# The residual's gate: products on ACT, POOL and DVE, summed over partitions by PE

## The chip, the cores and the metric

The kernel runs on one core of a Trainium2 chip. The metric is the device time of one execution in microseconds. Before the change the median of three runs is 2271.47 us (2270.25 to 2272.49).

The engines of a core are named as in the profile: PE multiplies matrices (PEld is its load of the stationary operand), DVE and ACT and POOL work element by element, and SP issues most of the DMAs. A tile has 128 partitions; a matmul sums over the partitions of its two operands, the other engines work along the free dimension of each partition.

## The reference

One layer of a diffusion backbone on 128 context tokens and 256 latent tokens, with 2048 channels in fp32. What matters here is the adaptive modulation: two conditioning vectors (`c_ctx` for the context tokens, `c` for the latent ones) go through SiLU and one matrix of 2048 x 6144, which gives a shift, a scale and a gate for each stream.

```python
mod_ctx = (jax.nn.silu(c_ctx) @ ada_w[l] + ada_b[l])[None, None, :]
mod_lat = (jax.nn.silu(c) @ ada_w[l] + ada_b[l])[:, None, :]
...
shift, scale, gate = jnp.split(mod, 3, axis=-1)
h = _rmsnorm(x, norm_g) * (1.0 + scale) + shift
out, S_fin = _mixer(h, S0, rows, *mixer_w)
return x + gate * out, S_fin
```

`_mixer` ends with `merged = sigmoid(m_a) * y_a + sigmoid(m_b) * y_b` and `merged @ w_o`, where `y_a` and `y_b` are projections of the two branches by `w_out_a` and `w_out_b`. The gate is the last third of the 6144 columns: two vectors of 2048, each a product of a vector of 2048 with a matrix of 2048 x 2048. It is needed only where the output of `w_o` is multiplied by it and added to the residual.

## The kernel before, in words

All 384 tokens are handled together, with channels on the partitions and tokens in the free dimension. Every fp32 matrix product of the mixer is made of three matmuls of rounded parts (`mm3`): a weight tile and a data tile are each split into a rounded high part (`split`: a cast on ACT, tile `whi`) and the rest (a subtraction on DVE, tile `wlo`), and high x high, high x low and low x high are summed in PSUM.

The weight stream `ds_` (class `Stream`) walks over pairs of 128 output columns. For each pair, SP loads two halves of 1 MB (tile `raw`, two buffers), each half is split in two parts (three buffers of `whi` and of `wlo`), and each part feeds 24 matmuls. A count, `cnt`, is one `mm3` of the stream, three matmuls. The stream can carry a side generator, `side`, which is advanced once every so many counts; whatever it gives to PE stands at that place in PE's order. The order on PE is the order in which the program is written. The instructions of the other engines, and the DMAs, are ordered by a planner, in the main by the order of the program, but an instruction may come earlier on its engine when its inputs and its buffer are there. Once planned, each engine goes through its instructions in order.

The end of the kernel goes like this. The projection of branch B (`d_ob`, eight pairs) runs under the last scans. `load_ya` reads branch A's 16 tiles back from DRAM and splits them (`yah`, `yal`). Then comes the projection of branch A (`add_oa`, tile `d_oa`): eight pairs of 32 counts, 256 counts or 768 matmuls. After each column group of 128, `consume` multiplies the result by `sma`, adds `omb`, and splits the sum into `m_hi` and `m_lo`. Last come the products with `w_o` in column groups of 512, 512, 512, 256 and 256 (`acc`, `accl`), and `res_cols`, which multiplies by the gate, adds the residual and takes the final norm.

The gate is computed as side work of the projection of branch A, by `gate_rows` (line 994), in four quarters of 512 columns. For a quarter, `ada_rows` (line 277) reads four pieces of 1 MB of the matrix (tile `raw_adag`, three buffers) and makes four fp32 matmuls with each, in which the stationary operand `condw_gate` holds the two conditioning vectors in two of 32 columns. The four matmuls of a piece go to four groups of 32 rows of one PSUM tile (`pg`). ACT copies them to `m5g`, whose last row holds the bias, which a DMA from POOL's queue has brought (line 284). `m5g` is split (`m5h`, `m5l`), and for each stream two matmuls with a 0/1 selector (`sel_r`, lines 1008 and 1009) sum the rows and spread the sum over the 128 partitions (`pgb`); ACT copies that into `gate`. A quarter is eight steps of the generator, and one step is taken every five counts, so the gate lies in the first 160 of the 256 counts.

```python
if self.side is not None and self.cnt % 5 == 0:
    if next(self.side, 0) == 0:
        self.side = None
```

Of the kernel before, what the change touches and what calls it, by code (L numbers as in the profile page):

```python
# [9 lines left out]
F32 = mybir.dt.float32  # L10
F32R = mybir.dt.float32r
AF = mybir.ActivationFunctionType
ALU = mybir.AluOpType
AX = mybir.AxisListType

P = 128
D = 2048
# [18 lines left out]
NSEL = 99  # L36
# [20 lines left out]
def hybrid_step(ctx, tc, cst, x_prompt, x_sample, state_f, state_b, c, c_ctx, ada_w, ada_b, norm_g,  # L57
                w_in, mu_prev, mu_next, w0, w2, a0, a2, k_k, k_a, r_k, lnx_g, lnx_b, conv_w,
                w_out_a, w_out_b, w_o, final_g, y_prompt, y_sample, ns_f, ns_b):
    nc = tc.nc  # L60
    V, S, G, TE = nc.vector, nc.scalar, nc.gpsimd, nc.tensor

    win = w_in[0].rearrange("(k p) n -> p k n", p=P)
    adaw = ada_w[0].rearrange("(k p) n -> p k n", p=P)
# [15 lines left out]
    def mm3(out, wh, wl, xh, xl, start, stop):  # L80
        TE.matmul(out, wh, xh, start=start, stop=False)  # L81
        TE.matmul(out, wh, xl, start=False, stop=False)  # L82
        TE.matmul(out, wl, xh, start=False, stop=stop)  # L83

    def split(src, shape, th, tl, pool, nm, rows=P):
        hi = pool.tile(shape, F32R, tag=th, name=f"{th}_{nm}")
        lo = pool.tile(shape, F32R, tag=tl, name=f"{tl}_{nm}")
        S.copy(hi[0:rows], src)  # L88
        V.tensor_tensor(lo[0:rows], src, hi[0:rows].bitcast(F32), ALU.subtract)  # L89
        return hi, lo  # L90
# [20 lines left out]
    class Stream:  # L111
# [21 lines left out]
        def run(self):  # L133
            p = 0
            while True:
                self.extend(p)
                if p == len(self.pairs):
                    yield 0
                    continue
                tag, view, cols, xs, consume, before = self.pairs[p]  # L140
                if before is not None:
                    before()
                xh, xl = xs()
                ps = []
                nt = len(cols)
                for i in range(nt):
                    pst = pd.tile([P, 512], F32, tag="d", name=f"d_{tag}_{i}")
                    ps.append(pst[:, 0:T])
                for half in range(2):
                    self.load(2 * p + half)  # L150
                    self.load(2 * p + half + 1)
                    wt = self.ready.pop(2 * p + half)
                    self.ready[2 * p + half] = None
                    for q in range(2):
                        hi, lo = wt[q]
                        for i in range(nt):
                            sl = slice(i * P, (i + 1) * P)
                            for kk in range(4):
                                k = 8 * half + 4 * q + kk
                                mm3(ps[i], hi[:, kk, sl], lo[:, kk, sl], xh[k], xl[k],  # L160
                                    k == 0, k == KC - 1)
                                if half == 1 and q == 1 and kk == 3:
                                    consume(i, ps[i])
                                    if i == nt - 1:
                                        self.done.add(tag)
                                self.cnt += 1
                                if self.side is not None and self.cnt % 5 == 0:
                                    if next(self.side, 0) == 0:
                                        self.side = None
                                yield 1  # L170
                p += 1
# [27 lines left out]
    cT = cp.tile([P, 32], F32, tag="cT", name="cT")  # L199
# [27 lines left out]
    for i in range(3):  # L227
        pr = pp.tile([P, P], F32, tag=f"prow{i}", name=f"prow{i}")
# [35 lines left out]
    def cond_weights(pool, nm):  # L264
        cw = pool.tile([P, KC, 32], F32, tag="condw", name=f"condw_{nm}")
        V.memset(cw[:], 0.0)
        for s in range(2):
            V.tensor_copy(cw[:, :, s], cT[:, 16 * s:16 * s + 16])
        return cw

    def ada_load(rp, nm, cols, i, rbufs):
        raw = rp.tile([P, 4, 512], F32, tag="araw", name=f"raw_ada{nm}_{i}", bufs=rbufs)
        o = 0
        for c0, w in cols:
            nc.sync.dma_start(raw[:, :, o:o + w], adaw[:, 4 * i:4 * i + 4, c0:c0 + w])
            o += w
        return raw

    def ada_rows(cw, m5, cols, ps, get):


        o = 0
        for c0, w in cols:
            nc.gpsimd.dma_start(m5[NSEL - 1:NSEL, o:o + w], ada_b[0:1, c0:c0 + w])
            o += w
        for j in range(4):
            raw = get(j)
            for kk in range(4):
                TE.matmul(ps[32 * kk:32 * kk + 32, 0:512], cw[:, 4 * j + kk, :], raw[:, kk, :], start=j == 0, stop=j == 3)
            if j == 3:  # L290
                S.copy(m5[0:NSEL - 1, :], ps[0:NSEL - 1, 0:512])
            yield 1

    condw = cond_weights(pp, "pro")
    sel = cs[0:NSEL, C_SEL:C_SEL + 2]
# [74 lines left out]
    for g in range(8):  # L370
        m5 = pp.tile([NSEL, 512], F32, tag="m5", name=f"m5_{g}", bufs=2)
        pa = pps.tile([P, 512], F32, tag="ada", name=f"pada_{g}")
# [592 lines left out]
    og = ctx.enter_context(tc.tile_pool(name="og", bufs=1))  # L965
    po_ = ctx.enter_context(tc.tile_pool(name="po_", bufs=2, space=bass.MemoryType.PSUM))
    gate = og.tile([P, 2, D], F32, tag="gate", name="gate")
    ctx_oa = ExitStack()
    oa = ctx_oa.enter_context(tc.tile_pool(name="oa", bufs=1))

    def load_ya():
        box["yah"] = Rows(oa, "yh", "yah")
        box["yal"] = Rows(oa, "yl", "yal")
        yload(ya_d, box["yah"], box["yal"], "a", lambda nm: oa.tile([P, T], F32, tag="yst", name=nm, bufs=3))

    load_ya()
    cw2 = cond_weights(oa, "gate")
    sel_r = oa.tile([NSEL, 2], F32R, tag="sel_r", name="sel_r")
    S.copy(sel_r[:], sel)
    gcols = [[(2 * D + 512 * q, 512)] for q in range(4)]  # L980
    graw = {}

    def gate_load(i):
        if i < 16:
            graw[i] = ada_load(oa, f"g{i // 4}", gcols[i // 4], i % 4, 3)

    gate_load(0)
    gate_load(1)
    m_t = {}

    def gate_rows():

        for q in range(4):
            m5 = oa.tile([NSEL, 512], F32, tag="m5g", name=f"m5g_{q}", bufs=2)
            pa = po_.tile([P, 512], F32, tag="pg", name=f"pg_{q}")

            def get(i):
                gate_load(4 * q + i + 2)
                return graw.pop(4 * q + i)

            yield from ada_rows(cw2, m5, gcols[q], pa, get)
            yield 1
            mh, ml = split(m5[:], [NSEL, 512], "m5h", "m5l", oa, f"{q}", rows=NSEL)
            yield 1
            for s in range(2):
                pb = po_.tile([P, 512], F32, tag="pgb", name=f"pgb_{q}_{s}")
                lhs = sel_r[:, s:s + 1].broadcast_to([NSEL, P])
                TE.matmul(pb[:], lhs, mh[:], start=True, stop=False)
                TE.matmul(pb[:], lhs, ml[:], start=False, stop=True)
                S.copy(gate[:, s, 512 * q:512 * q + 512], pb[:])  # L1010
                yield 1

    def add_oa(g):
        def before():
# [42 lines left out]
    for nq in range(3):  # L1057
        ns = slice(512 * nq, 512 * nq + 512)
        acc = []
        for s in range(3):  # L1060
            if nq % 2 == 0:
                a_ = pd.tile([P, 512], F32, tag="d", name=f"acc_{nq}_{s}")
            else:
                a_ = po_.tile([P, 512], F32, tag="pgb" if s else "pg", name=f"acc_{nq}_{s}")
            acc.append(a_)
        for q in range(4):
            raw = wp.tile([P, 4, 512], F32, tag="raw", name=f"raw_wo{nq}_{q}", bufs=2)
            nc.sync.dma_start(raw[:], wov[:, 4 * q:4 * q + 4, ns])
            for e in range(2):
                hi, lo = split(raw[:, 2 * e:2 * e + 2, :], [P, 2, 512], "whi", "wlo", wp, f"wo{nq}_{q}_{e}")  # L1070
                for s in range(3):
                    tsl = slice(s * P, (s + 1) * P)
                    for kk in range(2):
                        k = 4 * q + 2 * e + kk
                        mm3(acc[s][:], m_hi[k][:, tsl], m_lo[k][:, tsl], hi[:, kk, :], lo[:, kk, :],
                            k == 0, k == KC - 1)
        for s in range(3):
            res_cols(s, nq, 512 * nq, 512, acc[s][:])

# [2 lines left out]
    for half in range(2):  # L1082
        c0 = 1536 + 256 * half
        wt = []
        for q2 in range(2):
            raw = wp.tile([P, 8, 256], F32, tag="raw", name=f"raw_wl{half}_{q2}", bufs=2)
# [4 lines left out]
        for s in range(3):  # L1091
# [10 lines left out]
            if half == 1:  # L1102
                f = rsf[:, s, :]
# [37 lines left out]
```

## Time and profile before

| what | value |
|---|---|
| median of three runs | 2271.47 us |
| the profiled execution | 2274.91 us |
| its span, first to last instruction | 2273.1 us |
| mean granted TensorE clock | 0.994 |
| PE busy | 2201.9 us, 97% |
| DVE busy | 1539.6 us, 68% |
| ACT busy | 1012.6 us, 45% |
| POOL busy | 156.4 us, 7% |
| projection of branch A | 1974.90 to 2131.95 us of the span |
| loads of the gate's matrix | 16 of 1 MB, the first issued at 1935.5 us |

The profiled execution is one run of the program, and its time is a little above its span, since the span goes from the first to the last instruction. Busy time is the time in which an engine had an instruction under way. Lines of groups give the line, engine, operation, output and inputs, shape and count, then busy time, mean nanoseconds of one, and the idle time before them with what ended it. Lines of the timeline and of the chain of waits begin with the start in us from the span's start and the length in us.

### The profile page before, as it was taken

What the parts mean: (1) busy time and instruction counts of PE and PEld (TensorE: products, weight loads), DVE (VectorE), ACT (ScalarE), POOL (GpSimd) and SP (SyncE); (2) the same over time, 40 slices, a digit from 0 to 9 for tenths busy, and PEclk for the clock granted to TensorE, in tenths of its full rate; (3) what the DMA queues carried; (4) which work ended last, traced back from release to release, by engine and by line L of the source; (5) the groups of instructions that cost most, each with busy time, mean ns of one, the idle gap of its engine ahead of it and who ended that gap; (6) DMA issues with size and microseconds to landing.
All of it is one profiled execution on the core that took longest, in us unless ns stands there. A gap on an engine that the chain in (4) does not pass through costs nothing.

```text
span 2273.1 us, 40714 instructions
## 1 busy us (share of the span) xinstructions
PE 2201.9 (97%) x16084; PEld 2079.6 (91%) x16084; DVE 1539.6 (68%) x3096; ACT 1012.6 (45%) x1836; POOL 156.4 (7%) x131
## 2 busy tenths in 40 slices
PE   5999999999999999999999999999999999999998
PEld 3678999999999999999999999999999999889988
DVE  3259668787877877777869686777767684444444
ACT  4246345444444454444545454545454543333233
POOL 2001010101010101000010101010101000000000
PEclk9999999999999999999999999999999999999999
DMA  9963434444344444443534444444445465985633
GB/s 338 346 196 107 131 106 131 110 111 127 112 114 120 117 114 131 114 132 88 135 107 109 134 128 121 134 120 123 135 121 141 130 188 155 301 299 195 222 129 112
DMA packets 431694, 339.98 MB, mean 150 GB/s; under 512 B 86848, under 2 KB 413072, under 8 KB 430608
## 3 DMA queue, kind: packets, MB, share of 16 engines
q1 hardware_dynamic: 430016, 335.63, 50.0%
q8 instruction: 127, 2.08, 0.4%
q10 hardware_dynamic: 432, 1.57, 0.2%
q14 instruction: 63, 0.52, 0.1%
q0 software_dynamic: 1056, 0.19, 0.0%
HBM read 307.37 MB, written 29.36 MB: 148 GB/s over the span
## 4 chain that ended last, share of the span: by engine, by line
PE 79%; DVE 11%; DMA 6%; issue 2%; ACT 1%; SPq 1%; POOL 0%; POOLq 0%; DVEq 0%; ACTq 0%
DMA raw_adah<-in_ada_w_dram 4%; PE d_rk L81 3%; PE d_rk L83 3%; PE d_rk L82 3%; PE d_gv L81 3%; PE d_gv L82 3%; PE d_gv L83 3%; PE d_oa L81 2%; PE pA L689 2%; PE d_oa L83 2%; PE d_oa L82 2%; PE d_gb L81 2%; PE d_gb L83 2%; PE d_gb L82 2%; PE d_mb L81 2%
## 5 line engine op out<-in xcount | busy, mean ns | idle before, releaser
L713 DVE TENSOR_TENSOR ut<-U 48x30 f32<-48x30 f32 (+14 forms) x480 | 154.3, 322 | 18.8 <-DMA U<-ui 6.5
L81 PE MATMUL d_rk<-h_hi,whi_rk 128*128 128x384 f32 x480 | 163.2, 340 | 0.6 <-ACT lst L549 0.6
L81 PE MATMUL d_gv<-h_hi,whi_gv 128*128 128x384 f32 x480 | 161.0, 335 | 0.0
L715 DVE TENSOR_TENSOR U<-U,ut 48x30 f32<-48x30 f32 (+14 forms) x480 | 153.9, 321 | 10.3
L83 PE MATMUL d_gv<-h_hi,wlo_gv 128*128 128x384 f32 x480 | 160.8, 335 | 0.0
L82 PE MATMUL d_gv<-h_lo,whi_gv 128*128 128x384 f32 x480 | 160.7, 335 | 0.0
L82 PE MATMUL d_rk<-h_lo,whi_rk 128*128 128x384 f32 x480 | 160.5, 334 | 0.0
L83 PE MATMUL d_rk<-h_hi,wlo_rk 128*128 128x384 f32 x480 | 160.5, 334 | 0.0
L88 ACT CAST whi_gv<-raw_gv 128x1024 fp32r<-128x1024 f32 (+1 forms) x64 | 64.0, 999 | 140.6 <-PE d_rk L82 100.1
L89 DVE TENSOR_TENSOR wlo_rk<-raw_rk,whi_rk 128x1024 fp32r<-128x1024 f32 x60 | 73.0, 1219 | 61.1 <-ACT whi_rk L88 61.1
L88 ACT CAST whi_rk<-raw_rk 128x1024 fp32r<-128x1024 f32 x60 | 62.9, 1052 | 95.9 <-PE d_mb L82 18.0
L81 PE MATMUL d_bg<-h_hi,whi_bg 128*128 128x384 f32 x256 | 93.3, 364 | 2.4 <-DVE bc L462 2.4
L81 PE MATMUL d_bc<-h_hi,whi_bc 128*128 128x384 f32 x256 | 93.0, 363 | 0.0
L81 PE MATMUL d_ma<-h_hi,whi_ma 128*128 128x384 f32 x256 | 92.7, 362 | 0.0
L81 PE MATMUL d_mb<-h_hi,whi_mb 128*128 128x384 f32 x256 | 92.6, 362 | 0.0
L81 PE MATMUL d_bx<-h_hi,whi_bx 128*128 128x384 f32 x256 | 92.0, 360 | 0.0
L81 PE MATMUL d_ob<-ybh,whi_ob 128*128 128x384 f32 x256 | 89.1, 348 | 3.0 <-ACT ybh L503 1.3
L81 PE MATMUL d_gb<-h_hi,whi_gb 128*128 128x384 f32 x256 | 91.8, 359 | 0.0
L81 PEld LDWEIGHTS d_rk<-h_hi,whi_rk 128*128 128x128 f32 x480 | 90.1, 188 | 1.8 <-ACT lst L549 0.9
L81 PEld LDWEIGHTS d_gv<-h_hi,whi_gv 128*128 128x128 f32 x480 | 90.5, 189 | 0.1
L82 PEld LDWEIGHTS d_gv<-h_lo,whi_gv 128*128 128x128 f32 x480 | 90.4, 188 | 0.0
L83 PEld LDWEIGHTS d_gv<-h_hi,wlo_gv 128*128 128x128 f32 x480 | 90.4, 188 | 0.0
(320 smaller groups left out, 6620.3 us busy)
## 6 DMA issues: line engine op xcount, KB each, us to landing
raw_adah<-in_ada_w_dram SPq DMA_DIRECT2D x64, 512.0 KB, 8.7
raw_rk<-in_w_in_dram SPq DMA_DIRECT2D x60, 512.0 KB, 5.2
raw_gv<-in_w_in_dram SPq DMA_DIRECT2D x60, 512.0 KB, 4.9
raw_bc<-in_w_in_dram SPq DMA_DIRECT2D x16, 1024.0 KB, 5.5
raw_bx<-in_w_in_dram SPq DMA_DIRECT2D x16, 1024.0 KB, 5.4
raw_bg<-in_w_in_dram SPq DMA_DIRECT2D x16, 1024.0 KB, 5.5
raw_gb<-in_w_in_dram SPq DMA_DIRECT2D x16, 1024.0 KB, 5.5
raw_ma<-in_w_in_dram SPq DMA_DIRECT2D x16, 1024.0 KB, 5.7
```

The source lines that it names most:

```text
L81: TE.matmul(out, wh, xh, start=start, stop=False)
L82: TE.matmul(out, wh, xl, start=False, stop=False)
L83: TE.matmul(out, wl, xh, start=False, stop=stop)
L88: S.copy(hi[0:rows], src)
L89: V.tensor_tensor(lo[0:rows], src, hi[0:rows].bitcast(F32), ALU.subtract)
L689: TE.matmul(pas[h, n // 4 * 4][:, n % 4, :], bk[hss[h], n, :], pr[hss[h], n, :], start=True, stop=True)
L713: V.tensor_tensor(tv, U[:, 0:s, s:s + 1].broadcast_to([48, s, w]), U[:, s:s + 1, s + 1:].broadcast_to([48, s, w]), ALU.mult)
L715: V.tensor_tensor(U[:, 0:s, s + 1:], U[:, 0:s, s + 1:], tv, ALU.add)
```

## The change

The fp32 matmuls of the gate are taken away. For each of the 16 blocks of 128 rows of the matrix and each stream, the products are now formed along the partitions: row p of the block is multiplied by the conditioning value of that row, and the 16 blocks are added up, so that a tile of 128 x 512 stays whose sum over the partitions is the gate. For the first stream, ACT forms the product (`gpr`, two buffers) and POOL adds it to the accumulator; for the second, one DVE instruction multiplies and adds. The accumulator `gacc` (one buffer) is cleared by POOL, and its first partition starts from the bias, by two DMAs from POOL's queue. After 16 blocks it is split (`gah`, `gal`, one buffer each), and PE sums over the partitions and spreads the sum by two matmuls with a matrix of ones for each stream, in place of those with the selector. They stand in the seventh step of the next quarter, and those of the last quarter behind the first 512 columns of `w_o`. The matrix is read in 32 pieces of 512 KB, through five buffers, four of them loaded ahead. A quarter is again eight steps, of one piece each; a step is taken every seven counts instead of five, so that the 32 steps cover 224 of the 256 counts.

```diff
-                                if self.side is not None and self.cnt % 5 == 0:
+                                if self.side is not None and self.cnt % 7 == 0:
...
-    cw2 = cond_weights(oa, "gate")
-    sel_r = oa.tile([NSEL, 2], F32R, tag="sel_r", name="sel_r")
-    S.copy(sel_r[:], sel)
+    ones_r = og.tile([P, P], F32R, tag="ones_r", name="ones_r")
+    ones = oa.tile([P, P], F32, tag="gpr", name="ones", bufs=2)
+    V.memset(ones[:], 1.0)
+    S.copy(ones_r[:], ones[:])
...
     def gate_load(i):
-        if i < 16:
-            graw[i] = ada_load(oa, f"g{i // 4}", gcols[i // 4], i % 4, 3)
+        if i < 32:
+            q, k = divmod(i, 8)
+            graw[i] = oa.tile([P, 2, 512], F32, tag="araw", name=f"raw_adag_{i}", bufs=5)
+            nc.sync.dma_start(graw[i][:], adaw[:, 2 * k:2 * k + 2, 2 * D + 512 * q:2 * D + 512 * q + 512])
...
+    def gate_spread(q, gh, gl):
+        for s in range(2):
+            pb = po_.tile([P, 512], F32, tag="pgb", name=f"pgb_{q}_{s}")
+            TE.matmul(pb[:], ones_r[:], gh[:, s, :], start=True, stop=False)
+            TE.matmul(pb[:], ones_r[:], gl[:, s, :], start=False, stop=True)
+            S.copy(gate[:, s, 512 * q:512 * q + 512], pb[:])
...
     def gate_rows():
+        last = None
         for q in range(4):
-            m5 = oa.tile([NSEL, 512], F32, tag="m5g", name=f"m5g_{q}", bufs=2)
-            pa = po_.tile([P, 512], F32, tag="pg", name=f"pg_{q}")
...
-            yield from ada_rows(cw2, m5, gcols[q], pa, get)
-            yield 1
-            mh, ml = split(m5[:], [NSEL, 512], "m5h", "m5l", oa, f"{q}", rows=NSEL)
-            yield 1
+            ga = oa.tile([P, 2, 512], F32, tag="gacc", name=f"gacc_{q}")
+            G.memset(ga[:], 0.0)
             for s in range(2):
-                pb = po_.tile([P, 512], F32, tag="pgb", name=f"pgb_{q}_{s}")
-                lhs = sel_r[:, s:s + 1].broadcast_to([NSEL, P])
-                TE.matmul(pb[:], lhs, mh[:], start=True, stop=False)
-                TE.matmul(pb[:], lhs, ml[:], start=False, stop=True)
-                S.copy(gate[:, s, 512 * q:512 * q + 512], pb[:])
+                nc.gpsimd.dma_start(ga[0:1, s, :], ada_b[0:1, 2 * D + 512 * q:2 * D + 512 * q + 512])
+            for i in range(8):
+                gate_load(8 * q + i + 4)
+                raw = graw.pop(8 * q + i)
+                for kk in range(2):
+                    k = 2 * i + kk
+                    pr = oa.tile([P, 512], F32, tag="gpr", name=f"gpr_{q}_{k}", bufs=2)
+                    S.mul(pr[:], raw[:, kk, :], cT[:, k:k + 1])
+                    G.tensor_tensor(ga[:, 0, :], ga[:, 0, :], pr[:], ALU.add)
+                    V.scalar_tensor_tensor(ga[:, 1, :], raw[:, kk, :], cT[:, 16 + k:17 + k], ga[:, 1, :], ALU.mult, ALU.add)
+                if i == 6 and last is not None:
+                    gate_spread(q - 1, *last)
                 yield 1
+            last = split(ga[:], [P, 2, 512], "gah", "gal", og, f"{q}")
+        m_t["g"] = last
...
+        if nq == 0:
+            gate_spread(3, *m_t["g"])
         for s in range(3):
             res_cols(s, nq, 512 * nq, 512, acc[s][:])
```

More of the change, by code (lines that the diff above doesn't have):

```diff
@@ L976, in hybrid_step @@
     load_ya()
-    cw2 = cond_weights(oa, "gate")
-    sel_r = oa.tile([NSEL, 2], F32R, tag="sel_r", name="sel_r")
-    S.copy(sel_r[:], sel)
-    gcols = [[(2 * D + 512 * q, 512)] for q in range(4)]
+    ones_r = og.tile([P, P], F32R, tag="ones_r", name="ones_r")
+    ones = oa.tile([P, P], F32, tag="gpr", name="ones", bufs=2)
+    V.memset(ones[:], 1.0)
+    S.copy(ones_r[:], ones[:])
     graw = {}
     def gate_load(i):
-        if i < 16:
-            graw[i] = ada_load(oa, f"g{i // 4}", gcols[i // 4], i % 4, 3)
@@ L987, in hybrid_step @@
-    gate_load(0)
-    gate_load(1)
-    m_t = {}
+        if i < 32:
+            q, k = divmod(i, 8)
+            graw[i] = oa.tile([P, 2, 512], F32, tag="araw", name=f"raw_adag_{i}", bufs=5)
+            nc.sync.dma_start(graw[i][:], adaw[:, 2 * k:2 * k + 2, 2 * D + 512 * q:2 * D + 512 * q + 512])
+    for i in range(4):
+        gate_load(i)
+    m_t = {}
+    def gate_spread(q, gh, gl):
[4 more added lines that the diff above has]
+            S.copy(gate[:, s, 512 * q:512 * q + 512], pb[:])
@@ L991, in gate_rows @@
     def gate_rows():
+        last = None
         for q in range(4):
-            m5 = oa.tile([NSEL, 512], F32, tag="m5g", name=f"m5g_{q}", bufs=2)
-            pa = po_.tile([P, 512], F32, tag="pg", name=f"pg_{q}")
-            def get(i):
-                gate_load(4 * q + i + 2)
-                return graw.pop(4 * q + i)
-            yield from ada_rows(cw2, m5, gcols[q], pa, get)
-            yield 1
-            mh, ml = split(m5[:], [NSEL, 512], "m5h", "m5l", oa, f"{q}", rows=NSEL)
-            yield 1
```

## The prediction, made before the result was known

> **What bounds the kernel now.** I read the head of the page first, then the output stage in the windows, the waits of PE there, and the chain of waits in order of time.
>
> ```profile
> span 2273.1 us, 40714 instructions
> PE 2201.9 (97%) x16084; PEld 2079.6 (91%) x16084; DVE 1539.6 (68%) x3096; ACT 1012.6 (45%) x1836; POOL 156.4 (7%) x131
> ```
>
> PE is busy in 97% of the span. The stage of the change, the output projection of branch A (tile d_oa), is seen in two windows: the whole stage with all work, and one stretch behind the gate's last step that counts the d_oa work alone.
>
> ```profile
> 1974.90:2131.95 157.05, 157.05 (x916) 139.01 (x915) 65.16 (x82) 50.68 (x64) 0.97 (x2) 1.00 0.70 235
> 2081.20:2131.20 50.00, 50.00 (x290) 50.00 (x289) 3.31 (x6) 1.00 0.52 171
> ```
>
> The columns are the length, then busy time and count of PE, weight loads, DVE, ACT and POOL, the granted clock, DMA share and GB/s (the second row lacks ACT and POOL, which do no d_oa work). PE has no gap in these 157.05 us at clock 1.00; DVE is busy 41%, ACT 32%, POOL 1%. So here PE time is the kernel's time. One d_oa matmul costs 50.00 / 290 = 0.172 us. Where PE does wait near here is just before the stage:
>
> ```profile
> PE d_ob L81 <- DVE smb L516: 1.0, 1, 1.0
> PE d_ob L81 <- ACT whi_ob L88: 0.7, 1, 0.7
> PE d_ob L83 <- DVE wlo_ob L89: 0.6, 1, 0.6
> ```
>
> The chain shows what the gate takes of PE: the first two of its 16 row steps, the last, the last of its eight spread steps, and the start of the next stage.
>
> ```profile
> 1976.82 1.00 PE pg L289 x8
> 1977.81 0.38 PE d_oa L81
> 1980.64 0.99 PE pg L289 x8
> ...
> 2068.38 1.00 PE pg L289 x8
> ...
> 2080.50 0.23 PE pgb L1008
> 2080.72 0.23 PE pgb L1009
> 2131.95 0.23 PE acc L81
> ```
>
> **What is removed.** Between two row steps lie 1980.64 - 1976.82 = 3.82 us; 15 d_oa matmuls of these are 15 x 0.172 = 2.59, so a step costs 1.23 us: about 1.0 of fp32 matmuls on 32 columns, and a first d_oa matmul of 0.38 instead of 0.17 behind them. 16 steps: **19.7 us**. The whole stage agrees: 157.05 - 768 x 0.172 - 8 x 0.46 = 21. I take 19.7. Casts and copies of m5g (ACT and DVE, idle more than half of the stage) are hidden and bring nothing.
>
> **What stays on PE.** The spread stays 16 matmuls of 512 columns, at 0.23 us: 128 rows instead of 99 change nothing that the rows show. Two pairs move behind the first 512 columns of the last projection: cost 0. Their copies must leave the pgb banks before the accumulators of the next columns take them; one copy is 0.59 us (gate, below) and six acc matmuls of the first group cover 1.4 us: between 0 and 1 us, I take 1.
>
> **What is added.** 64 times: an ACT product, a POOL sum and a DVE multiply-add, each 128x512. The nearest rows:
>
> ```profile
> L88 ACT CAST whi_oa<-raw_oa 128x1024 fp32r<-128x1024 f32 x30 | 31.5, 1051 | 68.6 <-PE d_oa L82 65.4 <-PE d_ob L82 3.1
> L1010 ACT COPY gate<-pgb 128x512 f32<-128x512 f32 x8 | 4.7, 587 | 7.5 <-PE pgb L1009 7.1
> L613 ACT ACTIVATE kk<-k,par 128x384 f32<-128x384 f32 x16 | 9.9, 617 | 13.3 <-DVE k L419 13.3
> L1108 ACT ACTIVATE xr<-xr,rsf 128x1024 f32<-128x1024 f32 x3 | 3.5, 1153 | 4.3 <-POOL rsf L1106 4.3
> L89 DVE TENSOR_TENSOR wlo_oa<-raw_oa,whi_oa 128x1024 fp32r<-128x1024 f32 x30 | 36.7, 1224 | 72.5 <-ACT whi_oa L88 72.5
> L1027 DVE TENSOR_TENSOR sma<-sma,omb 128x384 f32<-128x384 f32 x15 | 8.4, 557 | 0.4
> L1029 DVE TENSOR_TENSOR m_lo<-sma,m_hi 128x384 fp32r<-128x384 f32 x15 | 8.3, 555 | 4.1 <-ACT m_hi L1028 4.1
> L776 DVE SCALAR_TENSOR_TENSOR kd<-kd,par,r 128x384 f32<-128x384 f32 x13 | 8.0, 613 | 0.3
> L1053 DVE TENSOR_TENSOR xr<-xr,fin 128x512 f32<-128x512 f32 x9 | 6.0, 686 | 0.1
> L705 POOL TENSOR_TENSOR bk<-bk,ep 128x768 f32<-128x768 f32 x32 | 51.6, 1613 | 165.4 <-PE pA L689 152.8 <-DMA yst_b<-yb_d 9.2 <-DMA ui<-A 3.3
> L579 POOL MEMSET s_in<- 128x128 f32 x2 | 0.3, 202 | 0.0
> L574 POOL MEMSET st<- 128x256 f32 x2 | 0.6, 312 | 38.9 <-PE pe L83 38.9
> ```
>
> ACT: scaling by a per-partition operand goes from 617 ns at 384 to 1153 at 1024 elements, so 0.72 us at 512; 64 are 46 us. DVE: 686 ns for a plain two-input form of 512, and up to 613 + 128 x 1.01 = 742 by the scalar form (1.01 ns an element from 384 to 512); I take 0.70, so 45 us. POOL: 1.50 us undisturbed for 768 elements (the rows below); without a fixed part that is 1.0 for 512, with the 0.09 that the two memsets leave it is 1.03. I take 1.03: 66 us. The memset and cast of ones stand in for those of the old selector, at 0. Beside these, four splits of 1024 elements (1.05 ACT, 1.22 DVE) replace four of 512. By busy time every engine has room in 157 - 20 = 137 us: ACT some 90, DVE some 110, POOL 70. The same 16.8 MB of weights come in halves, through five buffers instead of three; with a DMA share of 0.70 over the stage I cost this at 0 to 2 us, taking 0, because cover is lost only just before the stage, where the three waits above sit.
>
> **The price: POOL and DVE exclude each other.** POOL had 1% of this stage; elsewhere the timeline shows what happens when both read SBUF.
>
> ```profile
> 578.27 2.07 POOL L719 COPY UT<-U 48x1024 f32<-48x1024 f32 x1 [28.93 <-DVE U L715]
> 578.43 3.00 DVE L89 TENSOR_TENSOR wlo_bx<-raw_bx,whi_bx 128x1024 fp32r<-128x1024 f32 x1 [0.23 <-ACT whi_bx L88]
> ```
> ```profile
> 189.53 3.64 POOL L705 TENSOR_TENSOR bk<-bk,ep 128x768 f32<-128x768 f32 x1 [39.96 <-PE pA L689]
> 189.48 2.35 DVE L89 TENSOR_TENSOR wlo_bc<-raw_bc,whi_bc 128x1024 fp32r<-128x1024 f32 x2
> ```
> ```profile
> 1825.06 1.50 POOL L705 TENSOR_TENSOR bk<-bk,ep 128x768 f32<-128x768 f32 x1 [9.20 <-DMA yst_b<-yb_d]
> 1825.12 0.69 DVE L695 TENSOR_TENSOR A<-pA,cs 128x512 f32<-128x512 f32 x1
> 1825.72 2.18 DVE L504 TENSOR_TENSOR ybl<-yst_b,ybh 128x384 fp32r<-128x384 f32 x3
> 1944.27 1.58 DVE L504 TENSOR_TENSOR yal<-yst_a,yah 128x384 fp32r<-128x384 f32 x3 [2.82 <-ACT yah L503]
> ```
>
> First: the subtraction, 1.22 us alone, takes 3.00, and ends 1.09 us after POOL's copy. Second: the POOL product, 1.50 alone, takes 3.64, until two subtractions are through. Third: a DVE instruction with one operand in PSUM runs at its 0.69 beside POOL, while those with two SBUF operands (three take 1.58 alone, the last row) lose 0.6. So a DVE instruction with two SBUF operands and a POOL sum go one after the other; a DVE one holds the place for its record less 0.13. That is every DVE instruction here but the product with d_oa.
>
> The Trainium skill says the same as a rule (SBUF — State Buffer, Who interferes with whom): the pair of ports shared by the two engines is an exclusive lock, and whoever comes second blocks fully; this case's 3.00 against 1.22 agrees.
>
> Hold times: POOL 64 x 1.03 = 66; multiply-adds 64 x 0.57 = 36; weight subtractions 32 x 1.09 = 35; sma and m_lo 32 x 0.43 = 14; splits 4. Sum **155 us**, against 137 of PE. Part of it lies outside: the products need no PE, so the first may run when the first weights land, as POOL's bias loads for both the first quarters did before:
>
> ```profile
> 1934.84 1.09 POOL L284 DMA_DIRECT2D m5g<-in_ada_b_dram  x2 [8.79 <-DVE condw_gate L266]
> DMA to landing us min/median/max: 3.1/5.1/5.6
> ```
>
> That is 40 us ahead of the stage, and the last quarter is needed only after 144 acc matmuls (33 us) of the next one. So the place is nearly full, not overfull, and the order decides. ACT and DVE take their instructions in a fixed order: behind a product that waits for a POOL sum (two gpr buffers) stands the next cast of w_out_a, behind a multiply-add the next subtraction, and PE waits for these. Their cover: three whi/wlo pairs, 24 matmuls = 4.1 us each, so two stand ready, 8.3 us, less cast and subtraction (1.05 + 1.22): **5.9 us**.
>
> How late one quarter of the gate makes them: at best 0. At even odds, POOL holds the place 16.5 us of a quarter's 29 (56 counts of three matmuls), and some 33 DVE instructions (16 multiply-adds, 8 subtractions, 8 sma and m_lo, one split) meet it in 57% of cases and wait half of 1.03: 33 x 0.57 x 0.52 = 9.7 us, 3.8 past the cover. If POOL's sums are planned at their bare pace, 16.5 us, and every one queues behind DVE, 16 x (1.03 + 0.57) plus a third of the time for weights is 32 us: 15.5 late, 9.6 past the cover. Between quarters POOL clears one accumulator (0.1 + 1024 x 0.86 ns = 1 us) and waits 5.1 us for the bias rows, with the split and issue some 9 us, in which the casts and subtractions catch up. Four quarters: 0, 15 or 38 us. I take the middle of the first two, **7 us**, because the first two quarters have the 40 us of lead; 1 more for the moved spread.
>
> **Sum.** -19.7 + 7 + 1 = -11.7 us. The profiled execution took 2274.91 us around its span of 2273.1, and so 2263.2; it stands 3.4 above the median of the runs, 2271.47, which gives 2259.8, **2260**.
>
> **Rivals.** (a) The place is shared without harm: the lead and the cover take all. For it: ACT and DVE are idle over half of the stage now. Against: 155 us of holds. Then only 1 is lost: 2271.5 - 19.7 + 1 = 2253. (b) It costs what it saves, the 15 us and a few for the weights' DMA just before the stage: 2271.5 - 19.7 + 15 + 3 = 2270, no change. (c) Slower: the sums on POOL become the bound, at one place, gpr's two buffers. ACT stops at a product, casts of w_out_a behind it are late by 15.5 us a quarter, PE idles 9.6 of them: 2271.5 - 19.7 + 38 = 2290. It decides as soon as the loss passes 19.7, which is 4.9 us a quarter or 10.8 of lateness. For it: a POOL operation was seen waiting through two DVE ones. Against: only if the fixed order has the sums at their bare pace. (d) The change does not take the rows off PE's path, because PE waits for the spread instead. gah and gal are single, so a quarter's split waits for the spread of the one before; its sums may start once the spread two before it is done, 112 counts or 58 us of PE ahead of its own spread. A quarter at 32 + 9 us fits, so I give this no time of its own.
>
> By the exclusive lock of the Trainium skill's page (SBUF — State Buffer, Who interferes with whom) taken to the letter, with no room from the lead, (c) is the case; the trace has shown it only for single pairs of instructions, never for a stage.
>
> **How the numbers follow.** A measurement of this kernel tells about 0.2%, 4.5 us, from no change. Forecast 0.37, with a range of its own of 2256 to 2266; (a) 0.23; (b) 0.15; (c) 0.25. Faster is the forecast and (a): 0.60; same (b): 0.15; slower (c): 0.25. The range reaches from all of the gain, 2251, to most of (c): 2286.
>
> **What would show it.** Right: no pg matmuls, the stage near 137 us plus few PE gaps, each put down to whi_oa or wlo_oa; POOL sums of 1.03 us with a tail up to 2; DVE multiply-adds of 0.70 with a tail to 1.7. Wrong: PE gaps of 5 us and more in each quarter and ACT idle before gpr, waiting for POOL (c); no gaps at all (a); PE idle before pgb (d). A POOL sum far from 1.03 us alone, or multiply-adds that run beside POOL without delay, would fell the step on the price.

## The result and the profile after

The changed kernel takes **2306.59 us** (2303.34 to 2306.97), the kernel before, run beside it, 2271.95 us (2270.25 to 2272.49): a ratio of 1.0145, interval 1.0132 to 1.0158. It is 34.6 us slower, where the forecast was some 12 us faster and the range ended at 2286.

The head of the page of the changed kernel:

```profile
span 2304.3 us, 40801 instructions
PE 2197.8 (95%) x15956; PEld 2085.9 (91%) x15956; DVE 1641.7 (71%) x3158; ACT 1051.5 (46%) x1896; POOL 266.7 (12%) x203
```

The span grew by 2304.3 - 2273.1 = 31.2 us. PE lost its 128 row matmuls, yet its busy time fell by only 4.1 us. The windows (same columns as before) give the stage of branch A's output projection and, as the second row, 20 us of it:

```profile
1979.20:2162.10 182.90, 151.17 (x782) 145.01 (x782) 155.26 (x139) 83.33 (x113) 97.59 (x65) 0.92 0.62 202
2120.00:2140.00 20.00, 14.28 (x66) 13.78 (x67) 19.93 (x17) 10.64 (x16) 15.22 (x10) 0.74 0.48 145
```

The stage starts 1979.20 - 1974.90 = 4.3 us later than before and lasts 182.90 instead of 157.05 us, 25.85 more. What follows it is 31.2 - 4.3 - 25.85 = 1.05 us longer: the two pairs of the spread that were moved there are four matmuls of 0.23, 0.92 us. Inside the stage PE idles 182.90 - 151.17 = 31.7 us, where it had no gap. And its busy time is 151.2 us, where 157.05 - 19.7 - 0.92 = 136.4 were left to do: about **15 us** more for the same matmuls, with a granted clock of 0.92 instead of 1.00.

The waits of PE from 1920 us on (total, times, longest):

```profile
PE d_oa L83 <- DVE wlo_oa L89: 18.6, 10, 3.2
PE d_oa L81 <- DVE sma L1037: 11.9, 5, 6.5
PE d_ob L83 <- DVE wlo_ob L89: 4.6, 2, 3.9
PE d_ob L81 <- ACT whi_ob L88: 1.8, 1, 1.8
PE d_oa L81 <- ACT whi_oa L88: 1.2, 2, 0.7
```

Nearly all of it is put down to DVE: to its subtraction for the low weights, and to its product with d_oa, which frees the accumulator. The two waits in d_ob, 6.4 us against 1.3 for the same two lines before, lie just ahead of the stage. No wait names pgb, so the spread stops nobody.

Why DVE is late is read in the groups of instructions of that stage (count, then busy us, mean ns of one, idle before):

```profile
L1017 DVE SCALAR_TENSOR_TENSOR gacc<-raw_adag,cT,gacc 128x512 f32<-128x512 f32 x56 | 69.6, 1242 | 12.4 <-POOL gacc L1016 6.9 <-issue 2.5 <-DMA raw_adag<-in_ada_w_dram 1.1
L89 DVE TENSOR_TENSOR wlo_oa<-raw_oa,whi_oa 128x1024 fp32r<-128x1024 f32 x30 | 46.7, 1562 | 6.6 <-ACT whi_oa L88 6.6
L1038 DVE TENSOR_TENSOR sma<-sma,omb 128x384 f32<-128x384 f32 x15 | 17.0, 1133 | 0.2
L1040 DVE TENSOR_TENSOR m_lo<-sma,m_hi 128x384 fp32r<-128x384 f32 x15 | 13.0, 870 | 1.3 <-ACT m_hi L1039 1.2
L1037 DVE TENSOR_TENSOR sma<-sma,d_oa 128x384 f32<-128x384 f32 x15 | 8.2, 545 | 0.0
...
L1016 POOL TENSOR_TENSOR gacc<-gacc,gpr 128x512 f32<-128x512 f32 x56 | 91.7, 1638 | 47.2 <-ACT gpr L1015 34.9 <-DMA gacc<-in_ada_b_dram 8.5
```

Before, the subtraction took 1224 ns, the sum with omb 557 and m_lo 555; a multiply-add without sums beside it takes 752 (first experiment below). The stage therefore costs DVE 56 x 0.49 + 30 x 0.34 + 15 x 0.58 + 15 x 0.31 = 27.4 + 10.1 + 8.6 + 4.7 = **51 us** of waiting inside its own instructions. The product with d_oa, with one operand in PSUM, is untouched at 545 ns. DVE is "busy" 155 us in these rows, but 51 of them are waits.

Is it really DVE that PE waits for, or ACT behind it? The windows answer that. Nine waits of PE in the stage are longer than 1 us; here are the window of the longest and the sum over all nine (same columns; the sum has its means behind it):

```profile
2118.61:2125.12 6.51, 0.00 (x1) 0.01 (x1) 6.44 (x6) 3.75 (x5) 6.28 (x4) 0.50 0.47 142
sum 26.92, PE 0.04 PEld 0.04 DVE 26.67 ACT 10.44 POOL 16.71; mean PE 0.00 PEld 0.00 DVE 2.96 ACT 1.16 POOL 1.86
```

DVE is busy in 26.67 of these 26.92 us and ACT in 10.44, so what PE waits for is DVE's own queue. Once, ahead of the waits of 2.71 and 6.51 us, DVE had stood still itself:

```profile
2110.09 3.38 DVE L1017 SCALAR_TENSOR_TENSOR gacc<-raw_adag,cT,gacc 128x512 f32<-128x512 f32 x2 [6.86 <-POOL gacc L1016]
```

This is the start of the last quarter. POOL clears the one accumulator at 2102.16 and waits for the bias rows until 2108.58. ACT stops there too, for 8.15 us before gpr, with a cast of w_out_a behind it. No run gave the accumulator a second buffer.

The timeline of DVE, and then of POOL, in 11 us of the stage shows how the two meet (start, us, instruction):

```profile
2002.76 1.69 DVE L1017 SCALAR_TENSOR_TENSOR gacc<-raw_adag,cT,gacc 128x512 f32<-128x512 f32 x1 [2.47 <-issue]
2004.37 1.65 DVE L1038 TENSOR_TENSOR sma<-sma,omb 128x384 f32<-128x384 f32 x1
2005.94 1.78 DVE L1017 SCALAR_TENSOR_TENSOR gacc<-raw_adag,cT,gacc 128x512 f32<-128x512 f32 x1
2007.65 1.62 DVE L1040 TENSOR_TENSOR m_lo<-sma,m_hi 128x384 fp32r<-128x384 f32 x1
2009.19 0.54 DVE L1037 TENSOR_TENSOR sma<-sma,d_oa 128x384 f32<-128x384 f32 x1
2009.66 1.82 DVE L89 TENSOR_TENSOR wlo_oa<-raw_oa,whi_oa 128x1024 fp32r<-128x1024 f32 x1
2011.40 1.62 DVE L1038 TENSOR_TENSOR sma<-sma,omb 128x384 f32<-128x384 f32 x1
2012.95 0.74 DVE L1017 SCALAR_TENSOR_TENSOR gacc<-raw_adag,cT,gacc 128x512 f32<-128x512 f32 x1
...
2002.61 10.00 POOL L1016 TENSOR_TENSOR gacc<-gacc,gpr 128x512 f32<-128x512 f32 x6 [2.75 <-DMA gacc<-in_ada_b_dram]
```

While POOL's six sums run, 2002.6 to 2012.6, every DVE instruction with two SBUF operands takes 1.6 to 1.8 us, whether it needs 0.56 alone or 0.75 or 1.22. At 2012.95, with the sums over, the same multiply-add takes 0.74. In this stretch the two alternate: six sums and six such DVE instructions, one of each in turn. Each of the six is 0.6 to 1.1 us longer than alone, most of a sum of 1.29 us (the sum alone, e1 below), where half of a sum of 1.03 had been allowed.

The last reading is the clock. The timeline of PE around its longest wait, single matmuls:

```profile
2125.12 0.69 PE L81 MATMUL d_oa<-yah,whi_oa 128*128 128x384 f32 x1 [6.51 <-DVE sma L1037]
2125.60 0.52 PE L82 MATMUL d_oa<-yal,whi_oa 128*128 128x384 f32 x1
...
2129.76 0.52 PE L83 MATMUL d_oa<-yah,wlo_oa 128*128 128x384 f32 x1
2130.08 0.41 PE L81 MATMUL d_oa<-yah,whi_oa 128*128 128x384 f32 x1
2130.34 0.34 PE L82 MATMUL d_oa<-yal,whi_oa 128*128 128x384 f32 x1
2130.51 0.34 PE L83 MATMUL d_oa<-yah,wlo_oa 128*128 128x384 f32 x1
```

The records overlap, so their starts are what counts. Behind the wait of 6.51 us the matmuls start 0.32 us apart (2125.60 to 2129.76 are 13 steps), and only from 2130.3 on 0.172. The stage has six such stretches, of 6 to 17 matmuls, 65 in all, behind waits of 2.7 to 6.5 us; one more wait of 2.80 us has none behind it. 65 x 0.15 = 9.7 us; the first matmul behind each wait, at 0.4 to 0.7 us, is part of the rest of the 15. The Trainium skill states this as a rule (TensorE: Matmul & The Clock Gate, Why this matters for your kernels): gaps of PE above some 3 us bring it back to half of its clock. The 0.32 against 0.172 agrees; two of the six stretches stand behind waits of 2.71 and 2.94 us, a little under that length.

### The profile page after: what moved, and what is told of

The parts are those of the page before. It is cut to its first block, busy times and chain, and to the rows that moved or that the text cites. A ratio compares the mean times of both kernels' runs of the same rounds, so it can differ in the third digit from the quotient of the medians.

```text
span 2304.3 us, 40801 instructions
## 1 busy us (share of the span) xinstructions
PE 2197.8 (95%) x15956; PEld 2085.9 (91%) x15956; DVE 1641.7 (71%) x3158; ACT 1051.5 (46%) x1896; POOL 266.7 (12%) x203
## 4 chain that ended last, share of the span: by engine, by line
PE 72%; DVE 14%; DMA 7%; issue 4%; SPq 1%; ACT 1%; POOL 1%; POOLq 0%; DVEq 0%; ACTq 0%
PE d_rk L81 3%; PE d_rk L82 3%; PE d_rk L83 3%; DMA raw_adah<-in_ada_w_dram 3%; PE d_gv L82 3%; PE d_gv L81 3%; PE d_gv L83 3%; PE pA L689 2%; PE d_gb L81 2%; PE d_mb L81 2%; PE d_gb L82 2%; PE d_gb L83 2%; PE d_bc L81 2%; PE d_mb L83 2%; PE d_mb L82 2%
## 5 line engine op out<-in xcount | busy, mean ns | idle before, releaser
L908 POOL TENSOR_TENSOR rs<-var,nhalf 128x6 f32<-128x6 f32 x16 | 21.2, 1325 | 864.9 <-DVE var L906 864.9
L1016 POOL TENSOR_TENSOR gacc<-gacc,gpr 128x512 f32<-128x512 f32 x64 | 104.5, 1632 | 54.6 <-ACT gpr L1015 41.9
L83 PE MATMUL d_oa<-yah,wlo_oa 128*128 128x384 f32 x256 | 91.3, 357 | 18.6 <-DVE wlo_oa L89 18.6
L81 PE MATMUL d_oa<-yah,whi_oa 128*128 128x384 f32 x256 | 90.7, 354 | 13.1 <-DVE sma L1037 11.9
L719 POOL COPY UT<-U 48x1024 f32<-48x1024 f32 x16 | 38.2, 2385 | 477.6 <-DVE U L715 477.6
```

The lines of the kernel that those rows point to most:

```text
L719: G.tensor_copy(UT[:], U[:].rearrange("p a b -> p b a"))
L908: G.tensor_tensor(rs[:], var[:], nhalf[:], ALU.pow)
L1016: G.tensor_tensor(ga[:, 0, :], ga[:, 0, :], pr[:], ALU.add)
```

## The experiments

The theory tested first is that POOL's sums hold up DVE itself by their reads (theory L in the expectations). The rival is the prediction's (c): that the ring of two gpr buffers stops ACT, and with it the casts behind. Times are compared by ratio with the kernel before on the same chip, whose median was 2274.1 to 2274.6 us in these comparisons. Differences in us are those of the medians.

### e1: without the sums

```diff
-                    G.tensor_tensor(ga[:, 0, :], ga[:, 0, :], pr[:], ALU.add)
+                    if k == 0:
+                        G.tensor_tensor(ga[:, 0, :], ga[:, 0, :], pr[:], ALU.add)
```

> The changed kernel with 60 of POOL's 64 sums left out (one for each quarter stays), so the first stream's gate lacks 15 of 16 blocks; ACT's products and DVE's multiply-adds stay. Theory L (a POOL sum and a DVE instruction with two SBUF operands exclude each other, and DVE is thereby late with the weights): multiply-adds fall from a median of 1.31 us to 0.73, PE's 40 us of waits go, 2253 to 2260 us. Rival D (DVE has simply got 45 us too much work): multiply-adds may be shorter but the time stays above 2290. Rival R (ACT is held by the two gpr buffers): also fast, 2253 to 2260, as nothing then waits for POOL.

Measured: 2259.9 us, ratio 0.9934 (0.9919 to 0.9950). The tile view (min/median/max in ns, first and last start):

```profile
L1018 DVE SCALAR_TENSOR_TENSOR gacc<-raw_adag,cT,gacc x64: 737/752/1716, 1943.9 to 2099.5; 128x512 f32<-128x512 f32 x64
L1017 POOL TENSOR_TENSOR gacc<-gacc,gpr x4: 1285/1288/1292, 1944.6 to 2078.2; 128x512 f32<-128x512 f32 x4
```

60 sums are the whole loss and more: 2306.6 falls to 2259.9, by 47 us. The four that are left show the sum's own price, 1.29 us, and the multiply-adds theirs, 0.75.

### e2: POOL as busy, but writing only

60 sums became memsets of the gpr buffer, which is made wider for it, so that they take about as long as a sum (1.27 us at the median).

```diff
-                    pr = oa.tile([P, 512], F32, tag="gpr", name=f"gpr_{q}_{k}", bufs=2)
+                    pr = oa.tile([P, 704], F32, tag="gpr", name=f"gpr_{q}_{k}", bufs=2)
...
-                    G.tensor_tensor(ga[:, 0, :], ga[:, 0, :], pr[:], ALU.add)
+                    if k == 0:
+                        G.tensor_tensor(ga[:, 0, :], ga[:, 0, :], pr[:, 0:512], ALU.add)
+                    else:
+                        G.memset(pr[:].bitcast(mybir.dt.bfloat16), 0.0)
```

> The changed kernel with 60 of the 64 sums replaced by a POOL memset over the same gpr buffer, 1408 elements of two bytes, about 1.3 us each as a sum alone takes: POOL is as busy, gpr's ring is as slow, but POOL reads no SBUF. The first stream's gate lacks 15 of 16 blocks. Theory L, if only POOL's reads exclude DVE: 2253 to 2262, multiply-adds 0.73. Theory L, if its writes exclude DVE too: like the changed kernel, 2295 to 2310. Rival R (the ring): 2285 to 2300 although the multiply-adds take 0.73.

Measured: 2265.29 us, 0.9950 (0.9931 to 0.9968), 3 us above the range that theory L gave and 20 below that of the ring.

```profile
L1020 DVE SCALAR_TENSOR_TENSOR gacc<-raw_adag,cT,gacc x64: 734/750/1667, 1942.4 to 2100.3; 128x512 f32<-128x512 f32 x64
```

With POOL in the same ring at that pace, the multiply-adds run at 750 ns. So it isn't POOL's time, but what a sum reads, that holds DVE; the ring with a POOL instruction of that length costs about 2265.3 - 2259.9 = 5 us.

### e3: the sums without the multiply-adds

```diff
-                    V.scalar_tensor_tensor(ga[:, 1, :], raw[:, kk, :], cT[:, 16 + k:17 + k], ga[:, 1, :], ALU.mult, ALU.add)
+                    if k == 0:
+                        V.scalar_tensor_tensor(ga[:, 1, :], raw[:, kk, :], cT[:, 16 + k:17 + k], ga[:, 1, :], ALU.mult, ALU.add)
```

> The changed kernel with 60 of DVE's 64 multiply-adds left out, so the second stream's gate lacks 15 of 16 blocks; POOL's sums stay. Theory L: the sums still hold up subtractions and the work on sma, about 40 to 60 times by up to 1.1 us, but DVE has the 45 us and more of the multiply-adds free for it: 2255 to 2272. Rival R (the ring of gpr and ACT): still slow, 2285 to 2300.

Measured: 2286.58 us, 1.0044 (1.0028 to 1.0060). The theory had expected 2255 to 2272: a miss. ACT's waits (total, times, longest):

```profile
ACT gpr L1015 <- POOL gacc L1016: 42.5, 39, 7.6
```

Even with 60 of the multiply-adds gone, the remaining DVE work alternates with the sums: the subtraction, 1.22 alone, still has a mean of 1.63. ACT also waits for POOL 42.5 us. From this run alone the two could not be told apart.

### e8: e3 with five gpr buffers

The edit is that of e3 and of e5 (below) together.

> The kernel without the multiply-adds (60 of 64 left out; second stream's gate lacks 15 of 16 blocks) took 2286.6 us, with 42 us in which ACT waited for POOL at gpr and 37 us in which DVE waited for ACT's casts. Here it has five gpr buffers instead of two (four raw buffers). If the ring of gpr is what holds that kernel (theory R for it): 2262 to 2272. If DVE's own waits for the sums hold it (L): 2280 to 2288.

Measured: 2279.41 us, 1.0022 (1.0011 to 1.0034), just outside of what either theory had expected. Of e3's 26.7 us over e1, the five buffers took back 2286.6 - 2279.4 = 7 us (5 by the ratios); some 20 stay. There PE waits for sma (13.0 us) and wlo_oa (3.5), both of DVE, but ahead of PE's longest wait, of 6.06 us, DVE had itself been waiting:

```profile
2101.18 2.05 DVE L89 TENSOR_TENSOR wlo_oa<-raw_oa,whi_oa 128x1024 fp32r<-128x1024 f32 x1 [5.57 <-ACT whi_oa L88]
```

That cast stood on ACT behind four products, each of which had waited for a sum of POOL. ACT still waits 30.9 us for POOL in all. So with the multiply-adds gone the chain of rival (c), ACT stopped at gpr with a cast behind, is part of what is left, with five buffers too, and the 5 to 7 us are only a lower bound for it.

### e5: the change with five gpr buffers

```diff
-                    pr = oa.tile([P, 512], F32, tag="gpr", name=f"gpr_{q}_{k}", bufs=2)
+                    pr = oa.tile([P, 512], F32, tag="gp5", name=f"gpr_{q}_{k}", bufs=5)
...
-            graw[i] = oa.tile([P, 2, 512], F32, tag="araw", name=f"raw_adag_{i}", bufs=5)
+            graw[i] = oa.tile([P, 2, 512], F32, tag="araw", name=f"raw_adag_{i}", bufs=4)
```

> The changed kernel with five gpr buffers instead of two (and, for the room, four raw buffers instead of five). The sums stay, so does their exclusion of DVE. Theory L (DVE's instructions, each made to wait for one sum): 2298 to 2308, ACT's 45 us of waits for POOL fall, PE's waits for wlo_oa and sma stay. Rival R (ACT stopped by the two buffers, with the casts behind it): 2265 to 2285.

Measured: 2307.32 us, 1.0146 (1.0129 to 1.0162), the same as the change. The waits of ACT, and of PE, in e5:

```profile
ACT gpr L1015 <- POOL gacc L1016: 12.1, 6, 3.7
...
PE d_oa L81 <- DVE sma L1037: 24.2, 6, 7.3
PE d_oa L83 <- DVE wlo_oa L89: 7.3, 2, 4.3
```

In the change, ACT waits 45.3 us for POOL in 35 waits. Here 33 us of that are gone, and the time stays: PE waits for DVE as long as before, 31.5 us against 30.5. The run is not a clean one, since a buffer of the gate's weights was given up for it (three pieces are loaded ahead instead of four) and ACT's waits for those weights grew from 15.1 to 44.8 us. Taken with the windows above, in which DVE is busy while PE waits, it says that the ring is not what binds the change; rival (c) has the wrong place.

### e11: the accumulator of DVE's stream in PSUM

The multiply-adds read the weights from SBUF and their running sum from PSUM, in 14 of the 16 blocks of a quarter fully. The whole gate is computed, with as many instructions on each engine.

```diff
+            pa = po_.tile([P, 512], F32, tag="pacc", name=f"pacc_{q}", bufs=1)
...
-                    V.scalar_tensor_tensor(ga[:, 1, :], raw[:, kk, :], cT[:, 16 + k:17 + k], ga[:, 1, :], ALU.mult, ALU.add)
+                    V.scalar_tensor_tensor(ga[:, 1, :] if k == 15 else pa[:], raw[:, kk, :], cT[:, 16 + k:17 + k],
+                                           pa[:] if k else ga[:, 1, :], ALU.mult, ALU.add)
```

> The changed kernel, whole gate computed, but the second stream's accumulator lies in PSUM for 14 of the 16 multiply-adds of a quarter (the last one writes it back to SBUF), so these have one tensor operand in SBUF instead of two. Same instructions, same count on every engine. Theory L (two SBUF operands against POOL's reads): the multiply-adds fall from a median of 1.31 us to 0.75, and the time to that of the kernel without them or a little above it, 2284 to 2298. If DVE is late because of the number of its instructions: no change, 2303 to 2310.

Measured: 2290.99 us, 1.0074 (1.0055 to 1.0093), as expected: 16 us of the loss are taken back by the place of one operand. Some 31 us over e1 remain. The sums still take turns with the subtraction (mean 1.56 us) and with sma + omb (0.77), and in PE's longest wait, of 6.07 us, DVE is busy for only 58% of the time, having waited 2.54 us for a cast of ACT. How the 31 us divide between the two was not isolated.

```profile
L1018 DVE SCALAR_TENSOR_TENSOR pacc<-raw_adag,cT,pacc x56: 741/755/757, 1943.6 to 2125.0; 128x512 f32<-128x512 f32 x56
L1018 DVE SCALAR_TENSOR_TENSOR pacc<-raw_adag,cT,gacc x4: 761/1668/1730, 1940.6 to 2095.6; 128x512 f32<-128x512 f32 x4
```

This is the clearest pair of rows of the case: beside the same POOL sums, the same instruction takes 755 ns at the median, and at most 757, with its accumulator in PSUM, and 1668 in the four blocks that still read two operands from SBUF. The Trainium skill states it so (SBUF — State Buffer, Who interferes with whom): a DVE instruction with two SBUF inputs contends with a GpSimd one that reads SBUF, not with one that only writes it. Both halves are borne out, the second by e2.

### e4: both streams on DVE

The change without ACT's products and POOL's sums; the whole gate is computed.

```diff
-                    pr = oa.tile([P, 512], F32, tag="gpr", name=f"gpr_{q}_{k}", bufs=2)
-                    S.mul(pr[:], raw[:, kk, :], cT[:, k:k + 1])
-                    G.tensor_tensor(ga[:, 0, :], ga[:, 0, :], pr[:], ALU.add)
+                    V.scalar_tensor_tensor(ga[:, 0, :], raw[:, kk, :], cT[:, k:k + 1], ga[:, 0, :], ALU.mult, ALU.add)
```

> Both streams by DVE multiply-adds (128 instead of 64), no product on ACT, no sum on POOL; the whole gate is computed. Theory L: every multiply-add 0.73 us, DVE has about 65 + 90 = 155 us of work for a stage of 137 us plus some 40 us ahead of it and 33 behind, so PE waits 0 to 15 us: 2253 to 2268, faster than the changed kernel by over 35 us with twice the instructions. Rival D (too much work on DVE): slower than the changed kernel, over 2306.

Measured: 2268.95 us, 0.9976 (0.9965 to 0.9987), a microsecond above the range expected and some 38 us below the change. POOL had taken 64 multiply-adds' worth of work, 64 x 0.75 = 48 us, off DVE, and made it wait 51. But DVE alone is now too full for this one stage: 128 x 0.747 = 96 us beside some 65 of its own work, against 137. PE waits 9.4 us for it.

### e6 and e7: the gate over two stages, without and with POOL

e6 is e4 with two quarters of the gate under branch A's projection, at half of the pace, and two under the last projection, where their pieces come through two buffers. e7 is e6 with ACT's products and POOL's sums for one stream of the first two quarters.

```diff
-                                if self.side is not None and self.cnt % 7 == 0:
+                                if self.side is not None and self.cnt % 14 == 0:
...
-                ds_.side = gate_rows()
+                ds_.side = gate_rows((0, 1))
...
+            side = gate_rows((2 + nq,))
...
+                if side is not None:
+                    next(side)
```

> DVE does both streams, as in the run with DVE alone (2269), but two quarters lie under branch A's projection (one step in 14 counts) and two under the first two column groups of the last projection, each spread just ahead of its use; the whole gate is computed. If DVE's load in the one stage is what is left of the loss: PE's 9 us of waits there fall below 3 and DVE in the last stage goes from about 50% to 75%: 2253 to 2260, faster than the kernel before by 0.5 to 0.8%. If the last stage has no room for it: 2265 to 2280.

> The same two-stage kernel, but with the first stream's 32 products and sums of the two quarters under branch A's projection on ACT and POOL, as in the change; the whole gate is computed. Theory L: even at half the density each sum (1.29 us of the port) costs DVE more than the multiply-add (0.65) that it spares: slower than the run with both on DVE by 3 to 15 us, 2258 to 2272. If a sum on POOL is a help as long as the port is not full: faster by 1 to 5 us.

Measured: e6 2272.03 us, 0.9989 (0.9979 to 0.9998), e7 2295.72, 1.0091 (1.0076 to 1.0106). The 32 products and sums cost 24 us, more than the 3 to 15 expected. e6, the stage in the windows and its longest wait of PE:

```profile
1975.10:2109.30 134.20, 134.20 (x774) 133.84 (x773) 94.37 (x128) 44.22 (x51) 1.92 (x3) 1.00 0.65 212
...
PE acc L82 <- DVE wlo_wo L89: 12.2, 2, 10.9
```

Under branch A the forecast's saving is there in full: 134.2 us, no gap, clock 1.00. It is lost again in the last projection, where PE waits 12.2 us and 10.9 of them at once, until 2158.28, for a weight subtraction. ACT's cast for that subtraction was ready at 2144.69, and the subtraction starts at 2157.01. Here is the stretch between, in the windows:

```profile
2144.69:2157.01 12.32, 2.71 (x12) 1.89 (x11) 12.14 (x18) 3.43 (x7) 0.46 (x1) 0.81 0.52 162
```

DVE is busy in 12.14 of the 12.32 us: the subtraction stands in its order behind twelve multiply-adds, five operations of the residual's columns and the split of gacc. A first piece of the gate's weights had landed late, 14.5 us after its issue, behind 4 MB of residual and final gain in the same queue. But that was at 2125.5, some 20 us ahead, and what it did to this wait is only argued.

### e10: e6 with the gate's first two pieces ahead of the residual

```diff
+    g_in.update(pool=op, bufs=2, last=32)
+    gate_load(16)
+    gate_load(17)
     fg = op.tile([P, D], F32, tag="fg", name="fg")
```

> The two-stage kernel with DVE alone lost 12.2 us of PE time at the start of the last stage, where the third quarter's first piece landed 14.5 us after its issue, behind the 4 MB of the residual and the norm's weights. Here its first two pieces are issued ahead of those. If that queue was the cause: PE's waits there fall below 4 us and the time by 7 to 12 us, to 2258 to 2264. If DVE's work in the last stage is the cause: 2268 to 2274 as before.

Measured: 2270.4 us, 0.9980 (0.9968 to 0.9991), where 2258 to 2264 was expected if the queue was the cause, and 2268 to 2274 if DVE's work was. The longest wait for wlo_wo fell from 10.9 to 6.0 us, but four waits of 10.2 us in all remain, and the time is e6's. The result is that of the second case: the longest wait stands at the same place, with the subtraction again behind multiply-adds, the residual and the split.

### e9: three quarters under branch A, one under the last projection, DVE alone

e10 with a step every 9 counts under branch A, three quarters there, and the last quarter at one step per two weight parts.

```diff
-                                if self.side is not None and self.cnt % 14 == 0:
+                                if self.side is not None and self.cnt % 9 == 0:
...
-                ds_.side = gate_rows((0, 1))
+                ds_.side = gate_rows((0, 1, 2))
...
-                if side is not None:
+                if nq < 2 and e == 1:
                     next(side)
```

> DVE alone, three quarters under branch A's projection (a step in nine counts) and one under the last projection (a step in two of its weight parts, first pieces issued ahead of the residual). DVE's load in branch A's stage is 65 + 3 x 23 = 134 of 135 us, less what runs ahead of it. If that fits: PE waits under 3 us in both stages, 2254 to 2261, 0.6 to 0.9% faster than the kernel before. If not: 2262 to 2270, as with four quarters there.

Measured: **2256.13 us** (2254.02 to 2257.47), 0.9916 (0.9900 to 0.9932), with the whole gate computed. It beats both kernels.

```profile
1975.00:2110.00 135.00, 135.00 (x778) 134.65 (x777) 115.72 (x161) 45.12 (x53) 3.84 (x6) 1.00 0.74 242
...
PE d_ob L83 <- DVE wlo_ob L89: 1.5, 1, 1.5
PE acc L82 <- DVE wlo_wo L89: 0.8, 1, 0.8
```

DVE is busy 115.7 of the 135 us, none of it waiting for POOL, and PE is never stopped in the stage. The gain over the kernel before, 2274.26 - 2256.13 = 18 us, is nearly the 19.7 us that the row steps cost.

## Why the prediction was wrong

**Right.** The 19.7 us on PE: the stage without a gap is 134.2 us in e6 and 135.0 in e9, against 157.05. The ACT product: 0.72 us forecast, 0.723 at the median. That DVE instructions with two SBUF operands and POOL's sums exclude each other, and that the product with d_oa is spared: e11 and the 545 ns. That PE would not wait for the spread, (d). The multiply-add is 0.75 alone instead of 0.70, which adds 3 us to DVE. The 1 us for the moved spread fits the last stage, which is 1.05 us longer, by luck: it was meant for copies that hold up the accumulators, and 0.92 of the 1.05 are the moved matmuls themselves, which the stage before no longer has.

**The step that failed** is the price of that exclusion, where the prediction let 57% of DVE's instructions meet a sum "and wait half of 1.03", and then took 7 us for four quarters because the first two had a lead. Of its terms two were off and a third was missing.

First, the wait of one instruction. The sum is 1.29 us alone, not 1.03: the row of 768 elements it was scaled from has a broadcast one among its operands (ep), and no row had two plain ones. Whether that or the fixed part of 0.09 us, taken from memsets, misled the scaling is not shown; a two-input POOL instruction of a single column (L1106, a power, in the kernel before) took 0.56 us. And an instruction that meets the sums does not arrive at a random point of one. By the alternation above it queues behind the sum that started when the DVE instruction before it was through, and so waits for most of it: 1.65 - 0.75 = 0.9 us, where 0.52 was taken. The share that meets a sum was well guessed: the mean loss of a multiply-add, 0.49, is 54% of 0.9.

Second, the lead of the first quarters. DVE lost 51 us in the stage, 51 / 4 = 12.8 us a quarter, 6.9 past the cover of 5.9. By the prediction's own formula that is 27.6 us for four quarters, and PE's gaps in the stage are 31.7; another 4.3 came before the stage, where the lead was to help. The forecast had 7 for all of it. It had also counted the time between two quarters as one in which casts and subtractions catch up, while at the start of the last quarter ACT and DVE stood still for 8.15 and 6.86 us, with PE's longest wait behind that. The 4.3 are not the sums alone: in the profiles, branch A's stage starts at 1977.4 to 1980.8 in all eight kernels with ACT's products, e1 among them (1979.4, with a wait of 3.5 us for whi_ob), and at 1971.8 to 1976.1 in the five without.

Third, a term that was missing: PE's clock. The waits of 2.7 to 6.5 us left it at about half of its rate for 2 to 5 us, 15 us in all. This share is what the windows leave over of PE's busy time; the spacing of the matmuls gives 9.7 of it directly, and no run isolated it.

The sum with the measured terms: -19.7 + 31.7 + 4.3 + 15 = +31 us, the 31.2 by which the span grew (the moved spread adds to the last stage what the one before has lost). Since the 15 is a remainder, the sum closes by construction and is no proof of its terms.

**The rivals.** (c) had the sign and was 17 us from the time, but not the place: it wanted ACT stopped at gpr's two buffers. ACT does stop there, 45.3 us, but DVE is busy in 26.67 of the 26.92 us of PE's longer waits, and without most of ACT's wait for POOL the time is the same (e5). ACT's stop is seen to cost PE something where DVE has less to do (e8 and e11), 5 to 7 us of it by the buffers between e3 and e8. The 32 us a quarter behind (c)'s 38 do not follow from the terms given: 16 x 1.60 = 25.6 and a third of eight subtractions at 1.09 are 28.5, which would have made 24 us of it and 2276. (a) and (b) fell with the gaps. The lock "to the letter", which the prediction tied to (c), was nearer than its choice of even odds.

**Open.** In e3, how much of the remaining loss is ACT's stop and how much DVE's turns is only bounded, since ACT still waits with five buffers; the same holds for the 31 us that e11 keeps over e1. Which of the work that runs early (ACT's products, the sums, the weights' transfers) makes the stage start late was not isolated. Another order of DVE's work in the last projection, which e6 and e10 point to, was not tried by itself; e9 moves a quarter of the gate away from there as well. Why a wait of 2.80 us brought no slow stretch and one of 2.71 us did, no run tells.

## What to carry to other kernels

Work that is handed to POOL to relieve DVE is not free for DVE: each instruction of DVE with two SBUF operands that runs beside a stream of POOL reads waited for most of a POOL instruction of 1.29 us (0.75 became 1.65 us), and here 48 us taken off DVE brought 51 us of waiting. Before sharing out, sum what DVE still has to do with two SBUF operands in that stage; if it's much, leave the work on DVE and spread it over a longer stretch (e9), or put one operand in PSUM (e11, which took back 16 of the 47 us). A small delay that left PE idle for some 3 us mostly cost more than its length here, since PE came back at about half rate.

## What was not expected of the hardware

That the two engines took turns one for one in the stretch shown, whatever the lengths: a sum of 1.29 us kept a pace of 1.61 at the median while DVE's instructions of 0.56 and of 0.75 us alone all took 1.6 to 1.8. That one operand's place decides: 755 ns against 1668. That a POOL sum of two plain operands of 512 takes 1.29 us, when a product of 768 with a broadcast operand takes 1.50. And that the granted clock can fall to 0.74 over 20 us in a stage of a kernel that holds 0.99 over its span.
